# A scaled-copy kernel: input tiles of 15 tokens, whole-tile stores, and weights transposed on TensorE

## The chip, the cores and the metric

The kernel runs on one core of a Trainium2 chip. The metric is the device time of one execution in microseconds, the median of several runs. The profile shows one execution, in which times are counted from the first instruction (the span). TensorE is called PE, VectorE DVE, ScalarE ACT, GpSimd POOL and SyncE SP in it.

## The reference

Each of 16 x 1024 = 16,384 tokens has 512 float32 values and k = 2 weights. The output holds each token twice, once times each weight. The expert indices are an input but are not used.

```python
def reference(x, expert_indices, expert_weights):
    batch, seq, hidden = x.shape
    k = expert_indices.shape[-1]
    x_expanded = x[:, :, np.newaxis, :].repeat(k, axis=2)
    weights = expert_weights[..., np.newaxis]
    return (x_expanded * weights).astype(np.float32)
```

So 33.55 MB of x and 0.13 MB of weights are read, 67.11 MB are written, and there is one multiplication for each output element.

## The kernel before

The tokens stand in 128 partitions, and a tile of n tokens gives each partition n neighbouring tokens: partition p of a tile has the tokens p*n to p*n + n - 1 behind the tile's start. So a partition's part of x in a tile is one contiguous run of n x 2 KB in memory, and its part of the output one run of n x 4 KB. There are five tiles of 25 tokens a partition and a last one of 3 tokens, called z (25 x 5 + 3 = 128).

Loads of x are issued from ScalarE's queue (`load`, L76). Tile 0 comes in two pieces, of 9 and 16 tokens; then come z and tile 1, and tile i + 2 is loaded after the work on tile i, into one of two x buffers. The weights are issued from SyncE's queue (`weights`, L94, L96, L103) in three transfers, which put them straight into the order of the tiles: for tile 0, 128 rows of 200 B; for tiles 1 to 4, 512 rows of 200 B; for z, 128 rows of 24 B. `w_tile` holds all 256 weights of a partition's 128 tokens.

`emit` cuts a tile into two or three parts (`cuts`: 13 and 12 tokens for tiles 0 and 1, 9, 8 and 8 for the others). Each part is multiplied by `fill` and stored by one transfer from SyncE's queue (L152). All parts lie in one ring, `o_ring`, of 25 tokens a partition, so a part of a later tile waits until the store that last used its place is done. `fill` gives two thirds of a part's tokens to VectorE, up to four tokens in one `tensor_tensor` (L126; the weight is broadcast over 512 elements and the token over the two copies), and the rest to ScalarE, one `mul` of 512 elements for each output row (L116).

The order on each engine is that of the program. Waits between engines and transfers are placed by the framework from the tiles that the instructions read and write.

Of the kernel before, what the change touches and what calls it, by code (L numbers as in the profile page):

```python
# [1 line left out]

# [4 lines left out]


@with_exitstack
def kernel(  # L10
    ctx: ExitStack,
    tc: tile.TileContext,
    x: bass.AP,
    expert_indices: bass.AP,
    expert_weights: bass.AP,
    out: bass.AP,
):
    nc = tc.nc

    batch, seq, hidden = x.shape  # L20
    k = expert_weights.shape[-1]
    P = nc.NUM_PARTITIONS
    ntok = batch * seq
    assert ntok % P == 0
    A_TOTAL = ntok // P

    f32 = mybir.dt.float32
    row = k * hidden
    CH = 4


    groups = [25, 25, 25, 25, 25]
    TX = max(groups)
    LAST = 3
    FIRST = [9, 16]
    assert sum(groups) + LAST == A_TOTAL

    xf = x.rearrange("b s h -> (b s) h")
    of = out.rearrange("b s k h -> (b s) (k h)")
    wf = expert_weights.rearrange("b s k -> (b s) k")  # L40

    w_pool = ctx.enter_context(tc.tile_pool(name="w_pool", bufs=1))
    x_pool = ctx.enter_context(tc.tile_pool(name="x_pool", bufs=2))
    o_pool = ctx.enter_context(tc.tile_pool(name="o_pool", bufs=1))

    w_tile = w_pool.tile([P, A_TOTAL * k], f32)
    o_ring = o_pool.tile([P, TX * row], f32)

    def rows(of_all, done, T):
        return of_all[done * P : (done + T) * P, :].rearrange(  # L50
            "(p a) n -> p (a n)", a=T
        )


    if LAST:
        z_pool = ctx.enter_context(tc.tile_pool(name="z_pool", bufs=1))
        z_tile = z_pool.tile([P, LAST * hidden], f32)

    tiles = []
    done = 0  # L60
    for n in groups:
        tiles.append((done, n))
        done += n

    loaded = []

    def load(i):
        if i >= len(tiles):
            return
        done, n = tiles[i]  # L70
        x_tile = x_pool.tile([P, TX * hidden], f32)
        src = rows(xf, done, n)
        steps = FIRST if i == 0 else [n]
        for e, step in enumerate(steps):
            at = sum(steps[:e])
            nc.scalar.dma_start(  # L76
                out=x_tile[:, at * hidden : (at + step) * hidden],
                in_=src[:, at * hidden : (at + step) * hidden],
            )
            if i == 0 and e == 0:  # L80
                for g in range(3):
                    weights(g)
        if i == 0 and LAST:
            nc.scalar.dma_start(out=z_tile, in_=rows(xf, A_TOTAL - LAST, LAST))
        loaded.append(x_tile)


    T0 = groups[0]
    G = len([n for n in groups[1:] if n == T0])
    head = (1 + G) * T0  # L90

    def weights(e):
        if e == 0:
            nc.sync.dma_start(out=w_tile[:, : T0 * k], in_=rows(wf, 0, T0))  # L94
        elif e == 1:
            nc.sync.dma_start(  # L96
                out=w_tile[:, T0 * k : head * k].rearrange("p (g n) -> p g n", g=G),
                in_=wf[T0 * P : head * P, :].rearrange(
                    "(g p a) n -> p g (a n)", g=G, p=P
                ),  # L100
            )
        else:
            nc.sync.dma_start(  # L103
                out=w_tile[:, head * k :], in_=rows(wf, head, A_TOTAL - head)
            )

    def product(engine, o_tile, t, x_in, c, m):

        o = t * row
        if engine is not None:  # L110
            for e in range(m * k):
                out_e = o_tile[:, o + e * hidden : o + (e + 1) * hidden]
                in_e = x_in[:, e // k * hidden : (e // k + 1) * hidden]
                w_e = w_tile[:, c + e : c + e + 1]
                if engine is nc.scalar or engine is nc.any and (c + e) % 3 == 2:
                    nc.scalar.mul(out=out_e, in_=in_e, mul=w_e)  # L116
                else:
                    nc.vector.tensor_scalar(
                        out=out_e,
                        in0=in_e,  # L120
                        scalar1=w_e,
                        scalar2=None,
                        op0=mybir.AluOpType.mult,
                    )
            return
        nc.vector.tensor_tensor(  # L126
            out=o_tile[:, o : o + m * row].rearrange(
                "p (t k h) -> p t k h", t=m, k=k
            ),
            in0=x_in[:, : m * hidden]  # L130
            .rearrange("p (t h) -> p t h", t=m)
            .unsqueeze(2)
            .to_broadcast([P, m, k, hidden]),
            in1=w_tile[:, c : c + m * k]
            .rearrange("p (t k) -> p t k", t=m)
            .unsqueeze(3)
            .to_broadcast([P, m, k, hidden]),
            op=mybir.AluOpType.mult,
        )

    def fill(o_tile, x_in, c, m):
        v = m - m // 3
        for t in range(0, v, CH):
            u = min(t + CH, v)
            product(None, o_tile, t, x_in[:, t * hidden : u * hidden], c + t * k, u - t)
        product(nc.scalar, o_tile, v, x_in[:, v * hidden :], c + v * k, m - v)

    def emit(src, dst, c, cuts):
        for at, to in zip(cuts, cuts[1:]):
            o_tile = o_ring[:, at * row : to * row]  # L150
            fill(o_tile, src[:, at * hidden : to * hidden], c + at * k, to - at)
            nc.sync.dma_start(out=dst[:, at * row : to * row], in_=o_tile)  # L152

    for i in range(2):
        load(i)
    for i, (done, n) in enumerate(tiles):
        cuts = [0, 13, n] if i < 2 else [0, 9, 17, n]
        emit(loaded[i], rows(of, done, n), done * k, cuts)
        load(i + 2)
    emit(  # L160
        z_tile,
        rows(of, A_TOTAL - LAST, LAST),
        (A_TOTAL - LAST) * k,
        [0, LAST],
    )

# [1 line left out]
_INS = ['x', 'expert_indices', 'expert_weights']  # L168
_OUTS = [((16, 1024, 2, 512), 'float32')]


# [23 lines left out]
```

## Time and profile before

| | |
|---|---|
| median of 3 runs | 239.96 us (239.96 to 240.86) |
| the profiled execution's own time | 239.6 us |
| its span, first to last instruction | 237.8 us |
| VectorE busy | 99.1 us (42%), 29 instructions |
| ScalarE busy | 49.1 us (21%), 77 instructions |
| TensorE busy | none |
| data moved by DMA | 100.80 MB, mean 424 GB/s over the span |

The page divides the span into 40 slices of 5.9 us; each digit is the busy share of a slice in tenths. The DMA row is the mean share of the core's 16 DMA engines. A group of instructions has its line, engine, operation, output and input tile, shapes and count, then busy time in us and the mean duration of one in ns, then the idle time of the engine just before them and what ended it. In an issue row of the DMA, the last number is the time from the issue to the landing of the data, waiting in the queue included.

### The profile page before, as it was taken

The page shows a single profiled execution, that of the slowest core. Times are in us where ns is not written, and L with a number is a line of the kernel's source. Part 1 is how long each engine was busy: PE and PEld are TensorE (multiplying, and loading weights), DVE is VectorE, ACT ScalarE, POOL GpSimd, SP SyncE. Part 2 cuts the span into 40 slices and gives each one's busy share as a digit, 9 for nine tenths or more (in the row PEclk, how much of TensorE's full clock was granted, in tenths as well). Part 3 has the DMA queues.
Part 4 walks back from the last instruction along what each step waited for, and adds up shares of the span by engine and source line. Part 5 has one row for each costly group of instructions (what it writes and reads, how often), then busy time and mean ns, then how long its engine had stood idle before and what let it go on. Part 6 is the DMA issues. An engine that isn't in the chain of part 4 may idle for free.

```text
span 237.8 us, 214 instructions
## 1 busy us (share of the span) xinstructions
DVE 99.1 (42%) x29; ACT 49.1 (21%) x77; POOL 0.2 (0%) x4
## 2 busy tenths in 40 slices
DVE  0599600000069292089005964008292946823000
ACT  0008900000062160060005260004040540402000
POOL 0000000000000000000000000000000000000000
DMA  7999999999999999999999999999999999999996
GB/s 255 447 411 465 476 441 413 414 425 430 430 397 397 488 430 454 424 430 406 404 444 432 453 402 453 441 408 457 440 409 441 419 424 443 459 404 441 441 441 265
DMA packets 3841, 100.80 MB, mean 424 GB/s; under 512 B 1152, under 2 KB 1152, under 8 KB 1280
## 3 DMA queue, kind: packets, MB, share of 16 engines
q1 hardware_dynamic: 2832, 67.24, 65.7%
q10 hardware_dynamic: 1008, 33.55, 33.2%
q14 instruction: 1, 0.01, 0.0%
HBM read 33.69 MB, written 67.11 MB: 424 GB/s over the span
## 4 chain that ended last, share of the span: by engine, by line
DMA 68%; DVE 20%; issue 2%; ACT 1%; DVEq 0%; SPq 0%
DMA out_dram<-o_ring 65%; DVE o_ring L126 20%; DMA x_tile<-in_x_dram 3%; ACT o_ring L116 1%; DVEq L126 0%; SPq L152 0%
## 5 line engine op out<-in xcount | busy, mean ns | idle before, releaser
L126 DVE TENSOR_TENSOR o_ring<-x_tile,w_tile 128x4096 f32<-128x4096 f32 (+2 forms) x28 | 96.8, 3507 | 113.0 <-DMA out_dram<-o_ring 99.9
L116 ACT ACTIVATE o_ring<-x_tile,w_tile 128x512 f32<-128x512 f32 x74 | 46.5, 708 | 139.2 <-DMA out_dram<-o_ring 130.8
L116 ACT ACT_TABLE_LOAD x1 | 1.3, 1283 | 18.8 <-DMA x_tile<-in_x_dram 18.8
L126 DVE TENSOR_TENSOR o_ring<-z_tile,w_tile 128x2048 f32<-128x2048 f32 x1 | 2.3, 2292 | 4.3 <-DMA out_dram<-o_ring 4.3
L116 ACT ACTIVATE o_ring<-z_tile,w_tile 128x512 f32<-128x512 f32 x2 | 1.3, 713 | 8.3 <-DMA out_dram<-o_ring 8.3
L179 POOL MEMSET const-bfloat16-1.0<- 128x1 bf16 x1 | 0.1, 101 | 0.0
L179 POOL MEMSET const-uint8-127<- 128x1 uint8 x1 | 0.1, 101 | 0.0
L179 POOL MEMSET const-float32-0.0<- 128x1 f32 x1 | 0.1, 98 | 0.2 <-issue 0.2
L179 POOL MEMSET const-float32-1.0<- 128x1 f32 x1 | 0.1, 98 | 0.0
## 6 DMA issues: line engine op xcount, KB each, us to landing
x_tile<-in_x_dram ACTq DMA_DIRECT2D x4, 6400.0 KB, 31.5
out_dram<-o_ring SPq DMA_DIRECT2D x6, 4096.0 KB, 24.4
out_dram<-o_ring SPq DMA_DIRECT2D x3, 4608.0 KB, 30.0
out_dram<-o_ring SPq DMA_DIRECT2D x2, 6656.0 KB, 33.2
out_dram<-o_ring SPq DMA_DIRECT2D x2, 6144.0 KB, 44.3
x_tile<-in_x_dram ACTq DMA_DIRECT2D x1, 4096.0 KB, 17.6
x_tile<-in_x_dram ACTq DMA_DIRECT2D x1, 2304.0 KB, 8.1
out_dram<-o_ring SPq DMA_DIRECT2D x1, 1536.0 KB, 20.5
```

Of the source, the lines that this page charges most:

```text
L116: nc.scalar.mul(out=out_e, in_=in_e, mul=w_e)
L126: nc.vector.tensor_tensor(out=o_tile[:, o : o + m * row].rearrange("p (t k h) -> p t k h", t=m, k=k), in0=x_in[:, : m * hidden] .rearrange ...
L179: nc = _bacc.Bacc("TRN2", target_bir_lowering=False, num_devices=1)
```

## The change

The tiles are cut anew: eight tiles of 15 tokens and a z of 8 (15 x 8 + 8 = 128). Each tile is loaded by one transfer (30 KB a partition, 3.93 MB; tile 0 is no longer loaded in two pieces) and stored by one transfer (60 KB a partition, 7.86 MB). In place of the ring there are two output buffers of 60 KB a partition. The z load is issued after that of tile 1.

The products all have 512 elements. Of a tile's 30 output rows VectorE takes the first 18 with `tensor_scalar`, ScalarE the other 12 with `mul`; of z's 16 rows, 10 and 6.

The weights of the eight tiles are read as 128 rows of 960 B: row p holds the weights of the 120 tokens that follow each other from 120 p, that is of eight blocks of 15 tokens, and block 8 p + e belongs to tile g at partition q where g x 128 + q = 8 p + e. Four transfers on SyncE's queue bring in 32 rows each (`raw`), two more bring z's weights. GpSimd builds an identity matrix (`eye`). TensorE transposes each of the eight column blocks of `raw` (128 x 30) into PSUM, four at a time; VectorE copies each four into `turned` (30 x 1024) with the columns put in the order of the tiles; TensorE transposes the eight tiles' columns back (30 x 128 into 128 x 30), and VectorE copies the 128 x 240 result into `w_tile`. VectorE's and ScalarE's first products need that copy.

```diff
-    groups = [25, 25, 25, 25, 25]
+    groups = [15] * 8
     TX = max(groups)
-    LAST = 3
-    FIRST = [9, 16]
+    LAST = 8
...
-    o_pool = ctx.enter_context(tc.tile_pool(name="o_pool", bufs=1))
+    o_pool = ctx.enter_context(tc.tile_pool(name="o_pool", bufs=2))
...
-        steps = FIRST if i == 0 else [n]
-        for e, step in enumerate(steps):
...
+        nc.scalar.dma_start(out=x_tile, in_=src)
         loaded.append(x_tile)
...
+    def weights():
+        c = TX * k
+        G = len(groups)
+        H = G // 2
+        raw = t_pool.tile([P, G * c], f32)
+        turned = t_pool.tile([c, G * P], f32)
+        eye = t_pool.tile([P, P], f32)
+        for e in range(4):
+            at, to = e * P // 4, (e + 1) * P // 4
             nc.sync.dma_start(
+                out=raw[at:to, :], in_=rows(wf, 0, G * TX)[at:to, :]
             )
+        for e in range(2):
+            at, to = e * P // 2, (e + 1) * P // 2
             nc.sync.dma_start(
+                out=w_tile[at:to, G * c :],
+                in_=rows(wf, A_TOTAL - LAST, LAST)[at:to, :],
             )
+        nc.gpsimd.memset(eye, 1.0)
+        nc.gpsimd.affine_select(
+            out=eye, in_=eye, pattern=[[-1, P]], ...
         )
+        back = ps_pool.tile([P, G * c], f32)
+        for h in range(2):
+            mid = ps_pool.tile([c, H * P], f32, name=f"mid{h}")
+            for j in range(H):
+                e = h * H + j
+                nc.tensor.transpose(
+                    mid[:, j * P : (j + 1) * P], raw[:, e * c : (e + 1) * c], eye
+                )
+            nc.vector.tensor_copy(
+                out=turned.rearrange("c (q h j) -> c h j q", h=2, j=H)[:, h],
+                in_=mid.rearrange("c (j q) -> c j q", j=H),
+            )
+        for g in range(G):
+            nc.tensor.transpose(
+                back[:, g * c : (g + 1) * c],
+                turned[:, g * P : (g + 1) * P],
+                eye[:c, :c],
+            )
+        nc.vector.tensor_copy(out=w_tile[:, : G * c], in_=back)
...
     def fill(o_tile, x_in, c, m):
+        cut = round(m * k * 0.6)
+        for e in range(m * k):
+            out_e = o_tile[:, e * hidden : (e + 1) * hidden]
+            in_e = x_in[:, e // k * hidden : (e // k + 1) * hidden]
+            w_e = w_tile[:, c + e : c + e + 1]
+            if e < cut:
+                nc.vector.tensor_scalar(
+                    out=out_e,
+                    in0=in_e,
+                    scalar1=w_e,
+                    scalar2=None,
+                    op0=mybir.AluOpType.mult,
+                )
+            else:
+                nc.scalar.mul(out=out_e, in_=in_e, mul=w_e)
...
+    def emit(x_in, dst, c, n):
+        o_tile = o_pool.tile([P, TX * row], f32)
+        fill(o_tile, x_in, c, n)
+        nc.sync.dma_start(out=dst, in_=o_tile[:, : n * row])
...
-    for i in range(2):
-        load(i)
+    load(0)
+    weights()
+    load(1)
+    nc.scalar.dma_start(out=z_tile, in_=rows(xf, A_TOTAL - LAST, LAST))
     for i, (done, n) in enumerate(tiles):
-        cuts = [0, 13, n] if i < 2 else [0, 9, 17, n]
-        emit(loaded[i], rows(of, done, n), done * k, cuts)
+        emit(loaded[i], rows(of, done, n), done * k, n)
         load(i + 2)
```

More of the change, by code (lines that the diff above doesn't have):

```diff
@@ L28 @@
     row = k * hidden
-    CH = 4
-    groups = [25, 25, 25, 25, 25]
+    groups = [15] * 8
     TX = max(groups)
-    LAST = 3
-    FIRST = [9, 16]
+    LAST = 8
     assert sum(groups) + LAST == A_TOTAL
@@ L43 @@
     x_pool = ctx.enter_context(tc.tile_pool(name="x_pool", bufs=2))
-    o_pool = ctx.enter_context(tc.tile_pool(name="o_pool", bufs=1))
+    o_pool = ctx.enter_context(tc.tile_pool(name="o_pool", bufs=2))
     w_tile = w_pool.tile([P, A_TOTAL * k], f32)
-    o_ring = o_pool.tile([P, TX * row], f32)
     def rows(of_all, done, T):
@@ L52, in rows @@
         )
-    if LAST:
-        z_pool = ctx.enter_context(tc.tile_pool(name="z_pool", bufs=1))
-        z_tile = z_pool.tile([P, LAST * hidden], f32)
+    z_pool = ctx.enter_context(tc.tile_pool(name="z_pool", bufs=1))
+    z_tile = z_pool.tile([P, LAST * hidden], f32)
+    t_pool = ctx.enter_context(tc.tile_pool(name="t_pool", bufs=1))
+    ps_pool = ctx.enter_context(
+        tc.tile_pool(name="ps_pool", bufs=1, space=bass.MemoryType.PSUM)
+    )
     tiles = []
@@ L72, in load @@
         src = rows(xf, done, n)
-        steps = FIRST if i == 0 else [n]
-        for e, step in enumerate(steps):
[L75 to L78, printed above, removed]
-            )
[L80 to L95, printed above, removed]
+        nc.scalar.dma_start(out=x_tile, in_=src)
+        loaded.append(x_tile)
+    def weights():
[7 more added lines that the diff above has]
+            at, to = e * P // 4, (e + 1) * P // 4
+            nc.sync.dma_start(
+                out=raw[at:to, :], in_=rows(wf, 0, G * TX)[at:to, :]
+            )
+        for e in range(2):
+            at, to = e * P // 2, (e + 1) * P // 2
@@ L96, in weights @@
             nc.sync.dma_start(
[L97 to L100, printed above, removed]
-            )
-        else:
-            nc.sync.dma_start(
-                out=w_tile[:, head * k :], in_=rows(wf, head, A_TOTAL - head)
-            )
[L107 to L139, printed above, removed]
@@ L141, in fill @@
-    def fill(o_tile, x_in, c, m):
[L142 to L152, printed above, removed]
@@ new lines, in weights @@
+        for g in range(G):
[5 more added lines that the diff above has]
+        nc.vector.tensor_copy(out=w_tile[:, : G * c], in_=back)
+    def fill(o_tile, x_in, c, m):
+        cut = round(m * k * 0.6)
[10 more added lines that the diff above has]
+                    op0=mybir.AluOpType.mult,
+                )
+            else:
+                nc.scalar.mul(out=out_e, in_=in_e, mul=w_e)
@@ L159 @@
         load(i + 2)
     emit(
[L161 to L164, printed above, removed]
+        z_tile, rows(of, A_TOTAL - LAST, LAST), (A_TOTAL - LAST) * k, LAST
     )
```

7 lines of the change are left out of this document (added).

## The prediction

> **What bounds the kernel now.** I read the page's slices and queues first, then the stretches, then the chain, and last the start in order of time. Slices and queues of the page:
>
> ```profile
> DVE  0599600000069292089005964008292946823000
> ACT  0008900000062160060005260004040540402000
> DMA  7999999999999999999999999999999999999996
> q1 hardware_dynamic: 2832, 67.24, 65.7%
> q10 hardware_dynamic: 1008, 33.55, 33.2%
> ```
>
> The transfers are at 9 in all slices but the first and the last, while VectorE and ScalarE idle for most of the span. q1 is SyncE's queue (weights and stores), q10 ScalarE's (loads). The stretches (length, busy time of each engine, granted clock, DMA share, GB/s) say how full that is:
>
> ```profile
> 0.00:3.00 3.00, 0.00 (x0) 0.00 (x0) 0.20 (x4) 1.00 0.44 104
> ...
> 68.00:140.00 72.00, 39.63 (x12) 19.71 (x32) 0.00 (x0) 1.00 1.00 432
> 140.00:220.00 80.00, 40.59 (x13) 17.96 (x29) 0.00 (x0) 1.00 1.00 433
> 220.00:236.00 16.00, 0.00 (x0) 0.00 (x0) 0.00 (x0) 1.00 0.98 422
> 236.00:237.80 1.80, 0.00 (x0) 0.00 (x0) 0.00 (x0) 1.00 0.08 34
> ```
>
> From 68 to 220 us the share is 1.00 at 432 to 433 GB/s, with loads and stores mixed, and the stores alone at the end run at nearly the same. I take 433. The 33.55 MB of x and 67.11 MB of output then need 100.66 / 0.433 = 232.5 us. The span of 237.8 has 5.3 us above that: about 1.7 before the first byte (3.0 x (1 - 0.44)), 1.7 behind the last (1.8 x 0.92), and some 2 in slow first packets and small weight rows. The change moves the same bytes, so a gain can only come out of these 5.3 us, while any time in which both queues are empty is a loss in full. The chain that ended last agrees:
>
> ```profile
> DMA out_dram<-o_ring 65%; DVE o_ring L126 20%; DMA x_tile<-in_x_dram 3%; ACT o_ring L116 1%; DVEq L126 0%; SPq L152 0%
> ```
>
> Its 20% on L126 is no price: in those stretches the DMA share is 1.00, because the other half of the ring or a load is still moving. So the question is whether a queue always holds work. Now the start, in order of time, and the DMA issues of the first 26 us (size of one, us to landing):
>
> ```profile
> 0.72 0.89 ACTq L76 DMA_DIRECT2D x_tile<-in_x_dram  x2
> 0.73 0.38 SPq L94 DMA_DIRECT2D w_tile<-in_expert_weights_dram  x1
> 1.17 0.42 SPq L96 DMA_DIRECT2D w_tile<-in_expert_weights_dram  x1
> 1.64 0.50 SPq L103 DMA_DIRECT2D w_tile<-in_expert_weights_dram  x1
> ...
> 8.89 18.61 DVE L126 TENSOR_TENSOR o_ring<-x_tile,w_tile 128x4096 f32<-128x4096 f32 x5 [8.89 <-DMA x_tile<-in_x_dram]
> 18.79 1.28 ACT L116 ACT_TABLE_LOAD   x1 [18.79 <-DMA x_tile<-in_x_dram]
> 20.08 9.91 ACT L116 ACTIVATE o_ring<-x_tile,w_tile 128x512 f32<-128x512 f32 x16
> 25.12 191.68 SPq L152 DMA_DIRECT2D out_dram<-o_ring  x14
> 30.02 0.37 ACTq L76 DMA_DIRECT2D x_tile<-in_x_dram  x1
> ```
>
> ```profile
> out_dram<-o_ring SPq DMA_DIRECT2D x1, 6656.0 KB, 42.5
> x_tile<-in_x_dram ACTq DMA_DIRECT2D x1, 6400.0 KB, 33.9
> x_tile<-in_x_dram ACTq DMA_DIRECT2D x1, 4096.0 KB, 17.6
> x_tile<-in_x_dram ACTq DMA_DIRECT2D x1, 2304.0 KB, 8.1
> z_tile<-in_x_dram ACTq DMA_DIRECT2D x1, 768.0 KB, 19.1
> w_tile<-in_expert_weights_dram SPq DMA_DIRECT2D x1, 100.0 KB, 36.8
> w_tile<-in_expert_weights_dram SPq DMA_DIRECT2D x1, 25.0 KB, 5.3
> ```
>
> Before, the loads that need no compute (tiles 0 and 1, z: 13.9 MB) run until 2.19 + 33.9 = 36.1 us, and the first store and the next load are issued at 25.12 and 30.02. That is 6 us of cover. VectorE starts at 8.89 because only 9 tokens and the first 25 KB of weights are wanted.
>
> **The change part by part.**
>
> Prefetch. Two loads of 15 tokens and 8 of z are 38 x 0.262 = 9.96 MB, 23.0 us at 433 GB/s. Before, 13.9 MB took 32.1 of the 35.4 us from 0.72 to 36.1, so 3.3 us go for first byte, slow first packets, weights and completion; with fewer weight rows I take 3.0. The prefetch has landed at 26.7 and its last byte moved at about 26.3. From there on the queues live on store 0 and load 2, which both need tile 0 finished.
>
> When the weights land. The 100 KB transfer is 512 rows of 200 B, 32 rows on each of 16 DMA engines and a completion, and it took 36.8 us, to 38.0. From 6.0 (landing of the 25 KB) to 38.0 the load queue moved about as many pieces: 24 rows of three loads, some left of the first, a few of the load issued at 30.02, and the completions, 32 to 33 in all. So an engine takes one piece of each queue in turn, however small. Now four quarter loads of weights stand on SyncE's queue, each 2 rows of 960 B and a completion per engine. The first goes ahead of the first x row, the other 9 pieces alternate with the 8 rows of 30 KB of x tile 0 and its completion. They land with tile 0. That tile is 3.93 MB, 9.1 us; the first 2.36 MB before took 8.1, of which 5.45 are the rate, so 2.6 on top: 0.72 + 9.1 + 2.6 = 12.4 us. One turn later would be 13.5 (a row of 30 KB is 1.1 us), and 5 us if the small rows did not have to take turns.
>
> [...]
>
> From weights to w_tile: 8 transposes, a copy of 30 x 512 (a second one behind the second four), 8 transposes back, a copy of 128 x 240. No PE instruction is in this trace. Nearest rows:
>
> ```profile
> L126 DVE TENSOR_TENSOR o_ring<-x_tile,w_tile 128x4096 f32<-128x4096 f32 x17 | 74.9, 4423 | 98.1 <-DMA out_dram<-o_ring 84.9 <-DMA x_tile<-in_x_dram 8.9 <-issue 4.2
> L116 ACT ACTIVATE o_ring<-x_tile,w_tile 128x512 f32<-128x512 f32 x74 | 46.5, 708 | 139.2 <-DMA out_dram<-o_ring 130.8 <-issue 8.4
> L126 DVE TENSOR_TENSOR o_ring<-x_tile,w_tile 128x1024 f32<-128x1024 f32 x2 | 2.4, 1217 | 0.0
> L179 POOL MEMSET const-float32-1.0<- 128x1 f32 x1 | 0.1, 98 | 0.0
> ```
>
> A transpose lies between 0.10 (the MEMSET, the shortest instruction) and 0.71 (an ACTIVATE over 512); it streams 30 to 128 columns, nearer to the short end, so 0.3. A DVE copy goes by the two L126 rows: (4423 - 1217) / 3072 = 1.04 ns an element and 0.15 us fixed, so 0.68 and 0.40. The first copy lies beside the second four transposes. 8 x 0.3 + 0.68 + 8 x 0.3 + 0.40 and four hand-overs of 0.1 make 6.3 us; with 0.10 and 0.71 it is 3.1 and 12.8. The identity (a POOL memset and select) lies under the wait for the weights. w_tile stands at 12.4 + 6.3 = 18.7.
>
> Tile 0. ScalarE has 12 products: 9.91 / 16 = 0.62 each, 7.45, with the table load of 1.28 in line, as at 18.79, 8.7 us. VectorE has 18 tensor_scalar of 512 elements in place of tensor_tensor. Upper bound: the rate of L126, 0.15 + 512 x 1.04 ns = 0.68, 12.3 us; lower bound: the fixed part alone, 2.7. I take the middle, 0.42 and 7.5 us; then ScalarE ends last. First store issued at 18.7 + 8.7 = 27.4; from issue to first byte 1.0 us (0.72 to 1.7 at the start), so bytes move at 28.4. Stall: 28.4 - 26.3 = 2.1 us.
>
> Steady state. A load row is 30 KB, a store row 60 KB; in turns, 8 of each, load i+2 ends with store i after (3.93 + 7.86) / 433 = 27.2 us. Tile i+2 waits for both (two x and two o buffers), needs at most 12.3 us, and its store and next load are queued while the pair behind, 27.2 us, moves. If that cover went, up to 8.7 us a tile would show; it does not go. On VectorE and ScalarE the waiting tile holds only its successors. The last stores (18.2 us for a tile, 9.7 for z) hide z's 16 products of some 5 us. Whole-tile stores cost and save nothing, as 422 to 433 GB/s held for rows of 12 to 52 KB. The z load moves behind x tile 1, cost nothing: it is wanted last. Removed: 96 rows and more of small weight pieces; I take 0.3 us off.
>
> Sum: 237.8 + 2.1 - 0.3 = 239.6 of span; the profiled execution took 239.6 against its span of 237.8, so 1.8 around it: 241.4. That execution is 0.15% under the median of 239.96; 241.4 is 0.6% above the median. About 0.5%, 1.2 us, is what a measurement of this kernel can tell from no change.
>
> **The rivals.**
>
> Not slower: no stall. If the first store is issued before 25.3, bytes follow before the prefetch ends at 26.3. That takes 2.1 us out of my chain: transposes at 0.17 in place of 0.3 (16 x 0.13 = 2.1), or a table load done under the wait (1.3) and half of that. 237.8 - 0.3 + 1.8 = 239.3. [...] Against: ScalarE's table load did stand behind its wait before. The early weights are one way to it: at 5 us w_tile would be done at 11.3, tile 0 would start at 12.4, the first store at 21.1.
>
> A longer stall: VectorE at L126's rate per product. 18 x 0.60 (1217 / 2, chained) = 10.9 and 18.7 + 10.9 = 29.6, a stall of 4.3: 243.6. With transposes at 0.5 as well, 3.2 more: 246.8. For it: these are the only rows of VectorE here. Against: one operand less is read. [...]
>
> Faster: the stall is nil and the 2 us of slow first packets and small rows shrink by more than 1.2: 238.5. Against: the slow first packets belong to the start itself, which stays.
>
> **How the numbers follow.** Stall of about 1.2 to 3.5 us, forecast: 0.43, 240.8 to 243. No stall or under 1.2: 0.40, 239.0 to 240.8; 0.06 of it by weights that land near 5 us, the rest by short transposes or a hidden table load. Longer stall: 0.12, 243 to 247. Faster by over 0.5%: 0.05. Slower by over 0.5% is then 0.53 (all but a little of the forecast, and the longer stall), within 0.5% 0.42, faster 0.05. The range leaves out the 0.05 and the upper half of the longer stall: 239.0 to 244.5; the forecast's own is 240.8 to 243. The likeliest time is 241.4.
>
> **What would show it.** Slices of DMA below 9 between 24 and 31 us, and a dip in no later place; quarter loads landing near 12 us, close to tile 0; VectorE's first copy near 15, its first product near 19; SyncE's first store near 27.4 and load 2 beside it; a store and a load of 27 us each round; pairs with a share of 1.00 as before. Wrong if the weights land near 5, if the first store leaves before 25.3, if a product of VectorE takes 0.6, or if the share falls later, which would be a wait that I do not see.

## The result, and the profile after

The changed kernel takes 282.28 us (median of six runs, 281.64 to 282.75) against 240.20 us for the kernel before in the same comparison (239.81 to 241.14). The ratio is 1.174, with a 95% interval of 1.171 to 1.177: 42 us slower, where 241.4 us was forecast. The profiled execution has a span of 281.0 us, 43.2 more than the 237.8 of before.

The page of the changed kernel, its slices (7.0 us each) and DMA queues:

```profile
DVE  0049900007200091001900027000360006405000
ACT  0029900008200090001900028000360006404000
DMA  7997979999999999999999999999999999999995
GB/s 291 426 423 297 402 289 363 380 341 350 341 359 350 341 347 359 329 350 359 315 332 341 359 350 341 359 350 341 359 350 341 341 394 420 420 420 455 420 426 224
q1 hardware_dynamic: 1648, 67.24, 67.4%
q10 hardware_dynamic: 1296, 33.56, 30.1%
```

The DMA row stands at 9 almost throughout, as before, so the DMA engines are seldom idle. But the row of GB/s stands near 350 from the seventh slice to the 32nd. The queue rows say how much time that is, since their last figure is the time of the packets as a share of 16 engines' span. SyncE's packets took 0.674 x 281.0 = 189.4 us per engine, and 0.657 x 237.8 = 156.2 before: 33.2 more for the same 67.24 MB. ScalarE's took 84.6 and 78.9: 5.7 more. Together that is 38.9 of the 43.2 us. The engines were not waiting between packets; the packets themselves took longer.

The stretches of the changed kernel (length; busy time of PE, PE's loads, VectorE, ScalarE and GpSimd; granted clock, DMA share, GB/s) show where:

```profile
26.00:31.00 5.00, 0.00 (x0) 0.00 (x0) 5.00 (x14) 5.00 (x9) 0.00 (x0) 1.00 0.50 115
31.00:68.00 37.00, 0.00 (x0) 0.00 (x0) 6.90 (x19) 7.54 (x13) 0.00 (x0) 1.00 1.01 365
68.00:140.00 72.00, 0.00 (x0) 0.00 (x0) 18.39 (x47) 18.78 (x31) 0.00 (x0) 1.00 1.01 348
140.00:220.00 80.00, 0.00 (x0) 0.00 (x0) 14.43 (x36) 15.10 (x25) 0.00 (x0) 1.00 1.00 344
```

From 68 us on, a share of 1.00 carried 432 to 433 GB/s before and carries 344 to 348 here. The rounds show it too, in the timeline of ScalarE in the changed kernel (start, length, what ended the idle time before):

```profile
64.58 7.46 ACT L138 ACTIVATE o_tile<-x_tile,w_tile 128x512 f32<-128x512 f32 x12 [29.46 <-DMA out_dram<-o_tile]
...
201.03 7.46 ACT L138 ACTIVATE o_tile<-x_tile,w_tile 128x512 f32<-128x512 f32 x12 [26.77 <-DMA out_dram<-o_tile]
```

These are tiles 2 and 6, four rounds apart: (201.03 - 64.58) / 4 = 34.1 us a round for 11.79 MB, which is 346 GB/s. 27.2 us had been predicted.

The start, by contrast, went much as worked out. The timeline of the changed kernel's first 36 us:

```profile
13.30 0.34 ACTq L148 DMA_DIRECT2D z_tile<-in_x_dram  x1
13.67 1.28 ACT L138 ACT_TABLE_LOAD   x1 [13.67 <-DMA x_tile<-in_x_dram]
...
15.68 1.87 PE L108 MATMUL mid<-eye,raw 128*30 128x128 f32 x8 [15.68 <-DMA raw<-in_expert_weights_dram]
16.73 1.98 DVE L111 COPY turned<-mid 30x512 f32<-30x512 f32 x2 [16.73 <-PE mid L108]
...
18.77 1.05 PE L116 MATMUL back<-eye,turned 30*128 30x30 f32 x8 [1.22 <-DVE turned L111]
19.86 0.41 DVE L121 COPY w_tile<-back 128x240 f32<-128x240 f32 x1 [1.15 <-PE back L116]
20.30 8.08 ACT L138 ACTIVATE o_tile<-x_tile,w_tile 128x512 f32<-128x512 f32 x13 [5.35 <-DVE w_tile L121]
...
27.79 7.71 SPq L143 DMA_DIRECT2D out_dram<-o_tile  x2
27.80 0.35 ACTq L72 DMA_DIRECT2D x_tile<-in_x_dram  x1
```

And three of its groups (busy us, mean ns of one):

```profile
L138 ACT ACTIVATE o_tile<-x_tile,w_tile 128x512 f32<-128x512 f32 x96 | 59.6, 708 | 167.5 <-DMA out_dram<-o_tile 162.2
L130 DVE TENSOR_SCALAR o_tile<-x_tile,w_tile 128x512 f32<-128x512 f32 x144 | 57.6, 480 | 163.9 <-DMA out_dram<-o_tile 163.9
L111 DVE COPY turned<-mid 30x512 f32<-30x512 f32 x2 | 2.0, 1062 | 16.7 <-PE mid L108 16.7
```

The page groups packets by queue; the trace has every packet of the DMA with its start, size and duration. In the changed kernel a store row is one packet of 61,440 B and a load row one of 30,720 B. Where only stores or only loads move, they take 2.27 and 1.14 us (27 B/ns on each of 16 engines, 433 GB/s in all). Between 100 and 200 us the median store row takes 3.05 us. 726 of the 1,152 store rows are over 0.2 us slower than at the full rate, and so are 207 load rows; the time by which all rows exceed that rate comes to 40.3 us, when spread over 16 engines. In the kernel before it is none of 1,792 store rows, though loads and stores are mixed there as well. So the experiments had one question: what makes a store row slow beside a load?

Both queues are issued 0.01 us apart at 27.8 us, and from there the rows take turns in a strict order, which the packets' starts show. Here they are from 28 us on, sixteen at a time (one for each DMA engine), with the median us of each sixteen:

```
changed kernel:   load 2.34, store 2.27, load 1.14, store 2.79, load 1.14, store 2.82
```

The kernel before has no such order: any sixteen of its packets at 100 us hold 5 to 11 loads. Below, "in step" means that every engine alternates a load row and a store row of the same number (row r of a load fills the partition that row r of the store empties), and "load first" or "store first" says which of the two begins.

### The profile page after: what moved, and what is told of

Read it like the earlier page. It is cut to its first block, busy times and chain, and to the rows that moved or that the text cites. A ratio compares the mean times of both kernels' runs of the same rounds, so it can differ in the third digit from the quotient of the medians.

```text
span 281.0 us, 406 instructions
## 1 busy us (share of the span) xinstructions
PE 2.9 (1%) x16; PEld 2.0 (1%) x16; DVE 64.1 (23%) x157; ACT 64.7 (23%) x103; POOL 0.7 (0%) x6
## 3 DMA queue, kind: packets, MB, share of 16 engines
q1 hardware_dynamic: 1648, 67.24, 67.4%
## 4 chain that ended last, share of the span: by engine, by line
another core or an unknown queue 37%; DMA 33%; ACT 10%; DVE 8%; PE 1%; issue 1%; SPq 0%; ACTq 0%; DVEq 0%
DMA out_dram<-o_tile 29%; ACT o_tile L138 10%; DVE o_tile L130 8%; DMA raw<-in_expert_weights_dram 5%; DVE turned L111 1%; SPq L84 0%; ACTq L72 0%; PE back L116 0%; PE mid L108 0%; DVE w_tile L121 0%; DVEq L179 0%; DVEq L130 0%; ACTq L138 0%
## 5 line engine op out<-in xcount | busy, mean ns | idle before, releaser
L138 ACT ACTIVATE o_tile<-x_tile,w_tile 128x512 f32<-128x512 f32 x96 | 59.6, 708 | 167.5 <-DMA out_dram<-o_tile 162.2
L130 DVE TENSOR_SCALAR o_tile<-x_tile,w_tile 128x512 f32<-128x512 f32 x144 | 57.6, 480 | 163.9 <-DMA out_dram<-o_tile 163.9
L130 DVE TENSOR_SCALAR o_tile<-z_tile,w_tile 128x512 f32<-128x512 f32 x10 | 4.0, 482 | 10.7 <-DMA out_dram<-o_tile 10.7
L138 ACT ACTIVATE o_tile<-z_tile,w_tile 128x512 f32<-128x512 f32 x6 | 3.8, 710 | 10.5 <-DMA out_dram<-o_tile 10.5
L111 DVE COPY turned<-mid 30x512 f32<-30x512 f32 x2 | 2.0, 1062 | 16.7 <-PE mid L108 16.7
L108 PE MATMUL mid<-eye,raw 128*30 128x128 f32 x8 | 1.9, 415 | 15.7 <-DMA raw<-in_expert_weights_dram 15.7
L108 PEld LDWEIGHTS mid<-eye,raw 128*30 128x30 f32 x8 | 1.0, 138 | 16.0 <-issue 15.7
L116 PE MATMUL back<-eye,turned 30*128 30x30 f32 x8 | 1.1, 290 | 1.2 <-DVE turned L111 1.2
L116 PEld LDWEIGHTS back<-eye,turned 30*128 30x128 f32 x8 | 0.9, 214 | 1.7 <-DVE turned L111 1.7
```

Source lines behind the costliest of these rows:

```text
L108: nc.tensor.transpose(mid[:, j * P : (j + 1) * P], raw[:, e * c : (e + 1) * c], eye)
L111: nc.vector.tensor_copy(out=turned.rearrange("c (q h j) -> c h j q", h=2, j=H)[:, h], in_=mid.rearrange("c (j q) -> c j q", j=H),)
L116: nc.tensor.transpose(back[:, g * c : (g + 1) * c], turned[:, g * P : (g + 1) * P], eye[:c, :c],)
L130: nc.vector.tensor_scalar(out=out_e, in0=in_e, scalar1=w_e, scalar2=None, op0=mybir.AluOpType.mult,)
```

## Experiments: one part of the change at a time

All runs of this section and the next are one execution each, beside runs of the kernel before at 239.6 to 240.3 us on the same chip. "Slow" counts store rows over 0.2 us above the full rate.

**Whole-tile stores, cut in two.**

```diff
-        nc.sync.dma_start(out=dst, in_=o_tile[:, : n * row])
+        for at, to in ((0, 8), (8, n)):
+            if at < to:
+                nc.sync.dma_start(
+                    out=dst[:, at * row : to * row], in_=o_tile[:, at * row : to * row]
+                )
```

> After, but each tile's 60 KB row store is issued as two stores, of 8 and 7 tokens (32 and 28 KB a row), once the whole tile is multiplied; the loads, the buffers and the distance between the rows in memory stay. In after, loads alone and stores alone move at some 430 GB/s and both together at about 345. Theory LONG or RATIO (the 60 KB piece, or a store piece twice as long as the load piece it takes turns with, is what slows the mix): near 433 GB/s throughout, about 243 us. Theory PITCH (rows of 15 tokens lie in memory so that loads and stores collide): the mixed part still runs at 345, but less of each round is mixed, since the loads are done after half a store; six rounds of some 32 us in place of 34, about 269 us.

245.20 us; 19 slow rows of 2,176, and 433 GB/s from 68 to 220 us. So the loss hangs on the stores, and weights, transposes and the new products have no part in it. Two things changed at once, though: the rows are shorter, and the first part left at 27.11, 1.0 us ahead of the load at 28.15. The order became store, store, store, store, load, store.

**The parts in the other order**, meant to hold the step with short rows.

```diff
-        for at, to in ((0, 8), (8, n)):
+        for at, to in ((8, n), (0, 8)):
```

> The kernel with stores in two parts (which was fast), with the part of tokens 8 to 14 issued first; that part needs ScalarE's products too, so it is issued at the same moment as the load of tile 2, where before the first part left 1.0 us ahead. STEP: loads 2 and 3 run in step with the stores' parts, some 0.7 us lost on each of 16 rows, the stretch from 29 to 75 us well under 433 GB/s; later loads start beside a store that has begun, so out of step: 250 to 257 us. RATIO WITH ROW DISTANCE: pieces of about equal length, as fast as with the other order, 245 us.

244.71 us with 19 slow rows, but the step didn't come about: one part still left first, at 26.83, and the load 1 us later. It repeats the run above and tells nothing new.

**Tiles of 12 tokens.**

```diff
-    groups = [15] * 8
+    groups = [12] * 10
```

> After with ten tiles of 12 tokens in place of eight of 15: load rows of 24 KB, store rows of 48 KB. The ratio of 1 to 2 stays, the piece is shorter than before's 52 KB, the distance between rows is another. RATIO: still 345 GB/s in the mixed rounds, about 280 us. LONG: 433 GB/s, about 243 us. PITCH: another rate than 345 in the mixed rounds, either way.

283.62 us, as slow as with 15. Rows are 24 and 48 KB now, 977 of 1,408 store rows are slow, and the median one takes 2.46 us in place of 1.82. The first store and load left at the same time (both 25.26), load row first. So neither the number 15 nor the exact length or pitch of the rows is the cause.

**Loads from the stores' queue.**

```diff
-        nc.scalar.dma_start(out=x_tile, in_=src)
+        queue = nc.scalar if i < 2 else nc.sync
+        queue.dma_start(out=x_tile, in_=src)
```

> After, but the loads of tiles 2 to 7 are issued from SyncE's queue, each behind the store of the tile two before it, so that loads and stores go one after the other and not in turns. All three theories are theories of the mix (LONG, RATIO, PITCH): near 433 GB/s throughout, 243 to 246 us. If loads and stores taking turns is not the cause, the rounds stay at 34 us and the time near 280 us.

245.53 us, 430 GB/s, and 80 slow packets of the 1,920 of that queue. One queue holds a whole store, then a whole load; rows of 60 KB move at 2.27 us. The long row alone isn't it. It has to take turns with a load.

**The kernel before, with its loads cut in two** (13 and 12 tokens).

```diff
-        steps = FIRST if i == 0 else [n]
+        steps = FIRST if i == 0 else [13, 12]
```

> Before, but the loads of 25 tokens after tile 0 are cut into two of 13 and 12 tokens (26 and 24 KB a row), with the stores of 36 to 52 KB as they are: a load piece then takes turns with a store piece up to twice its length. RATIO: the mixed stretches fall towards 345 GB/s, 10 us or more longer, 250 to 260 us. LONG and PITCH: no change, 240 us.

242.70 us, 6 slow rows, 432 GB/s. Load rows of about half the store rows' length, in turns with them, cost nothing there: the ratio of lengths alone isn't it either. (By the count explained further below, no store row of this run was found right behind the load row of its own number.)

**Other memory.** Loads of tiles 2 to 7 come from 45 tokens earlier.

```diff
+        if i > 1:
+            src = xf[done * P - 45 : (done + n) * P - 45, :].rearrange(
+                "(p a) n -> p (a n)", a=n
+            )
```

> After, but the loads of tiles 2 to 7 read x from 45 tokens (three rows of 30 KB) further back in memory, so the partition that is loaded stays in step with the partition that is stored, while the place in memory that is read is another; these tiles' output is that of wrong tokens. STEP by the partition (or by the order of pieces in the engine): still 34 us a round, about 282 us. If what collides in step is the two places in memory: another rate, near 245 us if three rows are enough. RATIO WITH ROW DISTANCE: 282 us as well.

282.54 us and the same 726 slow rows. Where in memory the load row lies next to the store row makes no difference, as far as this one shift tells.

**The load of tile 2 issued behind the work on tile 1.**

```diff
-        load(i + 2)
+        if i > 0:
+            if i == 1:
+                load(2)
+            load(i + 2)
```

> After, but the load of tile 2 is issued only behind the work on tile 1, some 7 us later than the store of tile 0 beside which it stood; all sizes, buffers and later issues stay. Theory STEP: in after, a store and a load start at the same moment with 8 rows each on every DMA engine and take turns, so the engine always works on the same partition's row in both; a delay of 7 us (about three store rows) takes them out of step for the rest of the run, since the queues do not empty. Then near 433 GB/s, 244 to 248 us. Theory RATIO WITH ROW DISTANCE (30 KB rows against 60 KB rows, at these distances, whichever rows meet): still 34 us a round, about 283 us.

244.68 us, with 20 slow rows. The timeline, stretches and queues of this run:

```profile
27.83 7.72 SPq L143 DMA_DIRECT2D out_dram<-o_tile  x2
27.92 0.34 ACTq L72 DMA_DIRECT2D x_tile<-in_x_dram  x1
```

```profile
140.00:220.00 80.00, 0.00 (x0) 0.00 (x0) 25.70 (x64) 26.17 (x42) 0.00 (x0) 1.00 0.99 430
```

```profile
236.00:243.00 7.00, 0.00 (x0) 0.00 (x0) 0.00 (x0) 0.00 (x0) 0.00 (x0) 1.00 0.37 159
```

```profile
q1 hardware_dynamic: 1648, 67.24, 64.5%
q10 hardware_dynamic: 1296, 33.56, 32.4%
```

SyncE's packets are back at 0.645 x 243.0 = 156.7 us, those of before. But look at the first two rows: the load is not some 7 us late, as the edit was meant to make it. It left 0.09 us behind the store, in place of 0.01. That was enough to turn the order of the rows round, and nothing else about them changed:

```
changed kernel:   load 2.34, store 2.27, load 1.14, store 2.79, load 1.14, store 2.82
this run:         store 3.09, load 1.14, store 2.28, load 1.14, store 2.28, load 1.14
```

Both run in step through the whole steady state, with rows of the same 60 and 30 KB in the same two queues. Load first loses 38 us, store first next to nothing. That is the sharpest result of the study: one turn decides it. The other two runs that lost agree (tiles of 12 and other memory both began load, store, load, store).

## Experiments: the transfers alone

In the following runs nothing is computed: eight loads of 15 tokens, the eight stores and the last one of 8 tokens, of a buffer of ones, without weights and products. A small VectorE write sets which queue starts first. The loop is

```python
    for i, n in enumerate(groups):
        nc.scalar.dma_start(out=x_tiles[i % 4], in_=rows(xf, i * n, n))
        nc.sync.dma_start(out=rows(of, i * n, n), in_=o_tile)
```

**Load first, and store first.** In the second, the loads wait for a later VectorE instruction:

```diff
+    nc.vector.memset(late, 0.0)
     for x_tile in x_tiles:
-        nc.vector.memset(x_tile[:, :1], 0.0)
-    nc.vector.memset(o_tile[:, :1], 1.0)
+        nc.vector.tensor_copy(out=x_tile[:, :1], in_=late[:, :1])
```

> Transfers alone: no products and no weights. One 60 KB buffer is filled once and stored eight times as tiles of 15 tokens; eight tiles of x are loaded into four buffers; both queues start together, the load some 0.1 us ahead, and then hold work all the time (the output is not the product). In step from the first row: if the transfers by themselves make the loss, each round of 11.8 MB takes 34 us, 273 us for eight, and with the filling and z's store about 300 us. If it needs the products or the waits of after, 27 us a round, about 250 us.

> The transfers alone, with the store starting about 1 us ahead of the load, less than one store row: the engine then works on store row 0, load row 0, store row 1, load row 1, where with the load ahead it is load row 0, store row 0. Theory SAME ROW BEHIND (a store row is slow when it comes right behind the load into the same partition): about 250 us. Theory IN STEP (slow whenever both are within a row of each other): about 300 us.

The stretch from 140 to 220 us, load first and then store first:

```profile
140.00:220.00 80.00, 0.00 (x0) 0.00 (x0) 1.00 1.00 344
```

```profile
140.00:220.00 80.00, 0.00 (x0) 0.00 (x0) 1.00 1.01 423
```

303.98 us with 973 slow rows (of 1,152), against 268.84 with 139. The two queues are enough to make the loss; the compute engines aren't needed. The orders were load, store, load, store (2.31, 2.30, 1.14, 2.67 us) and store, store (on about a third of the engines one store more), then load and store in turns at 1.14 and 2.27. The second run's time lies between the two that were expected. Its slow rows make 7 us, and from 235 us on the engines finish unequally (a DMA share of 0.82 to 250 us, then of 0.24).

**Shorter store rows, load first.** Two stores of 8 tokens for each load of 15:

```diff
-        nc.sync.dma_start(out=rows(of, i * n, n), in_=o_tile)
+        for e in (2 * i, 2 * i + 1):
+            nc.sync.dma_start(out=rows(of, e * 8, 8), in_=o_tile[:, : 8 * row])
```

> The transfers alone on 128 partitions, load ahead by 0.1 us, but stores as sixteen tiles of 8 tokens (32 KB a row, 1.21 us) beside the loads of 30 KB: step kept, ratio about 1 to 1. If being in step is enough, store rows that come behind a load take 0.5 to 0.9 us more, the 64 of each engine together 30 to 55 us: 280 to 305 us. If the 1 to 2 ratio or the long row is needed as well: about 250 us.

The sixteen stores hold all 128 tokens of a partition, so the last store of 8 tokens falls away, here and in the next run.

250.32 us and not one slow row. The order was load, store, load, store, in step as in the run that lost, with rows of 30 and 32 KB. So load first in step isn't sufficient: the store row has to be long, or longer than the load row.

**Short rows of both.** Loads of 4 tokens beside stores of 8:

```diff
-    for i, n in enumerate(groups):
-        nc.scalar.dma_start(out=x_tiles[i % 4], in_=rows(xf, i * n, n))
-        nc.sync.dma_start(out=rows(of, i * n, n), in_=o_tile)
+    for i in range(16):
+        nc.scalar.dma_start(
+            out=x_tiles[i % 4][:, : 4 * hidden], in_=rows(xf, i * 4, 4)
+        )
+        nc.sync.dma_start(out=rows(of, i * 8, 8), in_=o_tile[:, : 8 * row])
```

> The transfers alone on 128 partitions, load ahead by 0.1 us, sixteen tiles with loads of 4 tokens (16 KB a row) and stores of 8 tokens (32 KB a row): in step, ratio 1 to 2 as in after, the store row as long as in the run with equal rows, which lost nothing. If the ratio in step decides: store rows some 0.4 us over 1.21, 250 to 265 us. If it takes a long store row (48 KB lost 0.64 us, 60 KB 0.77): 214 to 222 us (16.8 MB are loaded, half as much as in the others).

217.44 us, 1 slow row. It can't part "long" from "longer than the load row". Its rows are 8 and 32 KB (16.78 MB are read), one to four, not the one to two of the changed kernel. And the loads were two rows ahead: load, load, store, load, store. No run that began like that lost from the start, and no store row of this one was found right behind the load row of its own number, so the run tests neither theory.

**Do the two rows need the same partition?** Each transfer is cut into two of 64 rows. One kernel loads and stores even partitions (shown), the other loads even ones and stores odd ones (`o_tile[1::2, :]`):

```diff
+        for e in range(2):
+            half = slice(e * P // 2, (e + 1) * P // 2)
+            nc.scalar.dma_start(
+                out=x_tiles[(2 * i + e) % 4][0::2, :], in_=rows(xf, i * n, n)[half, :]
+            )
-        nc.sync.dma_start(out=rows(of, i * n, n), in_=o_tile)
+            nc.sync.dma_start(out=rows(of, i * n, n)[half, :], in_=o_tile[0::2, :])
```

> The transfers alone, load ahead, each tile's load and store cut into two of 64 rows, the loads into the 64 even partitions and the stores from the same 64 even partitions, so that each DMA engine has 4 rows of each in step. PARTITION (it is the shared partition that costs) and TURN (it is the order of turns, whichever partitions): slow, about 300 us. If 64 rows a transfer change the pairing, something else.

> As the run with even partitions on both sides, but the stores come from the 64 odd partitions: the turns are the same, and no partition is both loaded and stored. PARTITION: about 250 us. TURN: as slow as with even partitions on both sides, about 300 us.

Even and even: 271.62 us, 152 slow rows. Even and odd: 257.45 us, 22 slow rows. But both began load, load, store, load, not in step, and the rows drifted against each other. The pair was run again without the extra VectorE write ahead of the stores, so that they leave ahead of the loads (by 0.02 us, at 16.89 and 16.91):

```diff
-    nc.vector.memset(o_tile[:, :1], 1.0)
```

> The transfers alone, 64 even partitions loaded and the same 64 stored, as before, but with the store issued some 0.3 us ahead of the load in place of 0.1 us behind it. Without that lead the engines took load rows 0 and 1 before store row 0, so the two were a row apart and 1024 rows of store ran at 27 bytes/ns; with it they should start load 0, store 0. PARTITION and TURN: from the second row on store rows take 0.5 to 0.9 us more than their 2.27, at least until a wait on a buffer takes the queues out of step; 270 to 300 us.

> The same lead, with loads into the even and stores from the odd partitions. PARTITION: in step as well, but store rows at 2.27 us, about 250 to 257 us. TURN: the store rows take 0.5 to 0.9 us more, as with even partitions on both sides.

Both now began store, load, store, load: in step, store first. 265.01 us with 51 slow rows and 254.99 with 47. That is the order that loses next to nothing with the same partitions too, so the totals of this pair couldn't tell; it is one more case in which store first runs free. (The 10 us between the two are not slow rows. In the first run a few engines still move rows from 250 us to its end at 263.2, at a DMA share of 0.09.) A last pair put one short load and a store ahead to shift the order by a turn (shown with even partitions on both sides; in the other the added store, too, reads odd ones):

```diff
+    nc.sync.dma_start(
+        out=of[120 * P : 120 * P + 480, :].rearrange("(p a) n -> p (a n)", a=TX),
+        in_=o_tile[0 : P // 2 : 2, :],
+    )
+    nc.scalar.dma_start(out=x_tiles[3][: P // 4 : 2, :], in_=rows(xf, 0, TX)[: P // 8, :])
```

> The transfers alone, even partitions loaded and stored. The run with the lead of 0.3 us began store 0, load 0, store 1: not in step with the load ahead. Here one extra store of two rows for each DMA engine goes ahead on the store queue and one extra load of one row on the load queue, so that the turns should become load 0, store 0, load 1, store 1. PARTITION and TURN: from then on store rows take 0.4 to 0.9 us more than 2.27, 275 to 310 us.

> The same turns (load 0, store 0, load 1, store 1), loads into even and stores from odd partitions. PARTITION: store rows at 2.27 us, 250 to 260 us. TURN: as slow as even against even.

The stretch from 140 to 220 us, even and even, then even and odd:

```profile
140.00:220.00 80.00, 0.00 (x0) 0.00 (x0) 1.00 1.00 377
```

```profile
140.00:220.00 80.00, 0.00 (x0) 0.00 (x0) 1.00 1.01 415
```

279.62 us with 294 slow rows, and 268.85 with 89. These begin at full rate too (the added rows of 4.8 to 5.8 us spoiled the start), and the even pair becomes slow later on, as the order drifts. In the two pairs that were not in step, rows that share partitions lost more than rows that don't: 152 against 22, 294 against 89. That speaks for the partition, but such totals also depend on how often each order came up.

The traces allow a closer count. Most packets start within 0.1 us of the end of another one (2,449 of the 2,944 of the changed kernel). Taking that one as the packet ahead on the same engine puts the packets of a run into 16 chains. Small packets of 4 B, 16 for each transfer (384 for the 24 transfers of the changed kernel), divide each chain into transfers, and in these the rows can be numbered. So each store row of 60 KB can be sorted by what stands right ahead of it on its engine. Rows of transfers that don't count out are left out (15% and 10% here, up to 43% in the runs with full transfers). The three runs of each kind together:

| right ahead of the store row | even and even | even and odd |
|---|---|---|
| the load row of the same number | 388 rows, 289 slow | 388 rows, 27 slow |
| a load row of another number | 1,192 rows, 9 slow | 1,294 rows, 24 slow |
| a store row | 1,022 rows, 26 slow | 1,072 rows, 51 slow |

In the first line the turns are the same in both columns, load first; only the partitions differ. So the turns alone don't make a store row slow: it has to read the partition that the load row right ahead of it fills. The full transfers agree. Behind the load row of the same number 417 of 440 store rows are slow in the changed kernel, 495 of 528 with tiles of 12, and 527 of 572 in the transfers alone with the load first. In the run whose load left 0.09 us behind the store no store row stands there, and of 725 behind the load row one number before, 4 are slow. In the kernel before and in both runs with the stores in two parts none was found there either. The reverse costs nothing: of 728 load rows right behind the store row of the same number in the run with 0.09 us, 5 are slow.

Two things limit this. With rows of 30 and 32 KB all 1,024 store rows that follow a load stand behind the load row of the same number, and none is slow. And the 139 slow rows of the transfers alone with the store first are of another kind (73 of 175 behind the load row three numbers before, 52 of 124 behind a store row, and none of 512 behind the load row two before); their cause stays open.

**The same turns, the stores from other partitions.** The last run keeps full transfers and lets each store read two overlapping rows from each of partitions 0 to 63 (the buffer, `o_wide`, is 4 KB a partition longer for that):

```diff
-        nc.sync.dma_start(out=rows(of, i * n, n), in_=o_tile)
+        twice = bass.AP(
+            tensor=o_wide.tensor,
+            offset=o_wide.offset,
+            ap=[[o_wide.ap[0][0], P // 2], [1024, 2], [1, TX * row]],
+        )
+        nc.sync.dma_start(
+            out=rows(of, i * n, n).rearrange("(q h) n -> q h n", h=2), in_=twice
+        )
```

> The transfers of p1_dma_load_first with one thing moved: each whole-tile store takes its 128 rows of 60 KB from 64 partitions, two overlapping rows from each, so that the row that an engine stores next to a loaded row lies in another partition (descriptor r reads partition r / 2, the load's descriptor r writes partition r). Output of a constant buffer, no products and no weights. If the loss needs a load and a store of the same partition in turn, store rows go back to 2.27 us, nearly none is slow, and the span is 240 to 255 us (p5_dma_equal_rows, p4_dma_store_first: 248.5 and 267.1). If stepping in turns with rows of 60 KB is enough, whatever the partition, it stays at 295 to 305 us with 900 or more slow store rows (p1_dma_load_first: 302.2 and 973).

```profile
140.00:220.00 80.00, 0.00 (x0) 0.00 (x0) 1.00 0.99 298
```

355.35 us: neither theory's number. That row is the stretch from 140 to 220 us again. 942 store rows are slow, and the median one takes 3.66 us, slower than in any other run, while the median load row keeps its 1.14. So stores that read two overlapping rows from each of partitions 0 to 63 have a price of their own here, which covers what the run was to measure. Stores from 64 even or 64 odd partitions, one row from each, ran mostly at 2.27 us in the earlier pairs (22 to 294 slow rows a run); whether it is the place of the 64 partitions or the two rows in one of them that costs, the run can't tell. On the question put, the run is inconclusive.

## Why the prediction was wrong, step by step

**Where it failed: the steady state.** The step that failed is "in turns, 8 of each, load i+2 ends with store i after (3.93 + 7.86) / 433 = 27.2 us", with its ground, "Whole-tile stores cost and save nothing, as 422 to 433 GB/s held for rows of 12 to 52 KB". A round took 34.1 us. With the store first it took 27.7 (five rounds from 57.78 to 196.46 us, by the starts of ScalarE's products), and six rounds at that difference make the 38 us. The turns were foreseen, and the price of a row was carried over from a kernel whose rows never stood in step. From 0.01 us between two issues there came an order, load row first, in which a store row of 60 KB takes 3.05 us in place of 2.27. What the runs show of its cause is this: it needs both queues taking turns (with the loads on the stores' queue it was 430 GB/s and 245.53 us), the load row first (0.09 us in place of 0.01 removes 38 us), and it needs the store row to read the partition that the load row right ahead of it fills (289 of 388 slow, against 27 of 388 where it reads the partition beside that). It was seen only with store rows of 48 to 60 KB beside load rows of half of that (with rows of 32 KB, load first, none was slow). It doesn't need the compute engines (303.98 us without them), the tile of 15 (283.62 with 12) or that place in memory (282.54 with another). Why the engine slows, and whether the row's length or its ratio to the load's decides, stays open.

None of the rivals held this case, and the range ended at 244.5. The text named "the share falls later" as the sign of an unseen trouble. The share never fell. It was the wrong view: the share counts time on packets and read 1.00 at 344 GB/s as at the 433 of before; GB/s and the packets' durations told slow ones from quick.

**The prefetch and the stall: right.** The prefetch's last packet ended at 26.9 (predicted 26.3), the next one began at 28.8 (28.4). That is a stall of 1.9 us, against 2.1.

**When the weights land: the mechanism right, the size off.** The last quarter landed at 15.54, not at 12.4: two turns of an x row of 1.14 us behind tile 0, which landed at 13.28, where they had been put level with it. (The text counts 96 rows and more of small weight pieces as removed; by the packets it is 512, 768 before and 256 after. No run shows the 0.3 us that was taken off for them.) One row of each queue at a turn, as the rows of 2.27 and 1.14 us alternate later, agrees with the 15.54; weights near 5 us, the rival's case, did not come.

**From weights to w_tile: 4.6 us instead of 6.3.** From 15.68 to 20.28. Eight transposes took 1.87 and 1.05 us, 0.23 and 0.13 each, below the 0.3 that was taken. The copy of 30 x 512 took 1.06 us where 0.68 was taken from the tensor_tensor rows; the copy of 128 x 240 took 0.41 (0.40). The four hand-overs took 0.02 to 0.04 each; the 0.1 put for each was the author's estimate.

**Tile 0: 7.5 us instead of 8.7.** The table load ran at 13.67, under the wait for the weights, and not in line as before. It waited only for x, and x came 2.3 us ahead of the weights. VectorE's products take 480 ns each and start 0.40 us apart (18 in 7.22), against the 0.42 taken. The rival of a longer stall needed 0.60 and fell. In the kernel before, half of a tensor_tensor of 1024 took 0.59 from start to start (1.17 us for the whole), 1.5 times as long as a tensor_scalar of 512. The errors of the last three steps cancel (3.1 us late, then 1.7 and 1.2 early): the first store left at 27.79, and 27.4 was predicted, so that the stall came out right is in part luck.

**The sum without the failed step.** With store first the same kernel takes 244.68, still 3.3 over the forecast. The stretch from 236 to 243 us of that run, above, has a share of only 0.37. By the packets the engines ended at 238.8 to 239.4 us and one alone at 241.8, two rows of z behind: about 2.7 us. (In the kernel before all ended between 236.1 and 236.7.) The first store rows at 3.09 us cost another 0.8. Neither was in the sum. No version of the changed kernel is under the kernel before, 240.14 beside it; the best, 244.68, is 1.9% slower.

## What to carry to other kernels

A DMA share of 1.00 isn't full speed: here it stood beside 433 GB/s and beside 344. Read GB/s with it, and take each queue's share times the span: where that sum grows for the same bytes, as here from 235.1 to 274.0 us, the packets have become slower. Where a load and a long store of the same partitions are issued in the same moment, each round, look at which row goes first, and let the store go first or stagger them, so that no store row follows right behind the load row of its own partition: here such a row was slow in 417 of 440 cases in the changed kernel, and a difference of 0.08 us between the issues made 282.28 us or 244.68. A change that makes all transfers equal can build a rhythm that an uneven kernel never had.

## What the runs showed of the hardware that was not expected

- The order of two rows of the same partition on a DMA engine decided their speed: with rows of 30 and 60 KB in turns, 344 GB/s with the load first and 430 with the store first, from a difference of 0.08 us between the issues. A store row of 60 KB right behind the load row of its own partition was slow in 289 of 388 cases, right behind that of the partition beside it in 27 of 388, and a store row of 32 KB in none of 1,024.
- A turn on a DMA engine was one row, up to 60 KB in one packet (2.27 us alone), and the order of the first round held through the steady state, in which both transfers have as many rows on each engine (8).
- Stores that read from partitions 0 to 63 alone, two rows from each, took 3.66 us a row of 60 KB (the median), with loads at 1.14 beside them.
- The z load was issued at 13.30, not behind tile 1's load at 1.7: it waited until about the time tile 0 landed, 13.28. It cost nothing here.
